# A hybrid decoder trunk on one core: the first two FFN chunks interleaved, x on another queue, idle matmuls at the start, and GpSimd off the tensor work

## The chip, the cores and the metric

The kernel runs on one NeuronCore of a Trainium2 chip. The metric is the device time of one execution in microseconds (us); less is better. Everything is computed in float32, with the large matmuls done in float32r on pairs of high and low parts.

## The reference

Two layers over a sequence of 256 tokens with 1024 features; each adds four sub-layers to h:

```python
h += 0.5 * SwiGLU_1(rms(h))                # 1024 -> 2 x 2816 -> 1024
h += W_out [ A | B | C ](rms(h) @ W_in)    # parallel head groups:
#  A: gated DeltaNet, 4 heads x 128: causal conv on q/k/v, per-head decay,
#     a triangular inverse in each chunk of 64
#  B: dilated sliding-window attention, 4 heads x 64
#  C: causal spatial gating, 4 groups x 64: layer_norm(v), tril(w) @ v, times u
h += CrossAttn(rms(h), rms(mem))           # 4 heads into 256 memory tokens
h += 0.5 * SwiGLU_2(rms(h))
```

A last RMSNorm follows the second layer. The sub-layer with A, B and C is called the mixing stage here.

## The kernel before

**Data.** h is kept transposed: four tiles `hP` (rows `one<-xT`) of two 128-feature blocks by 256 tokens. The weights stream from HBM in pieces of 128x1024 float32 (`wr`, four buffers). `wsplit` makes each piece into a high part `wh` by a ScalarE cast and a low part `wl` by a subtraction, on VectorE or, where the caller says so, on GpSimd. `gained` does the same for x: `X` holds both parts of one 128-feature block times its gain, eight blocks for eight k tiles. `mm2` takes two matmuls for a k tile: `wh` against both parts of X (512 columns) and `wl` against the high part (256). Where parts can't be paired, three matmuls of 256 do it. Results land in PSUM tiles `pg` (four banks, `gbank`) or `ps` (four banks, `sbank`).

**The FFN.** 22 chunks of 128 hidden features. A chunk has a gate half and an up half of eight k tiles each, so 16 pairs of matmuls. `pend` holds two chunks ahead; `evac` reads a chunk's PSUM, applies the row factors `rbh` and SiLU, and splits the product. The row factors come from `Stats`: ScalarE squares (`t<-one`), VectorE adds them up, a matmul with ones sums over partitions (`ps<-one,t`, 128x1), VectorE makes `rv`, GpSimd takes the power -0.5 (`rch<-rv`), VectorE refines it, and a matmul spreads it over the partitions (`ps<-one,rch`).

**The start.** All loads are on SyncE's queue: the gains, then x and the first chunk's weights by turns. The first chunk alone is done k tile by k tile (`wi[0] == 0`); its weights are laid out for that on the host.

**Mixing.** After the row factors come the scalars of the decay (`zz`, `po`, small VectorE rows), six convolution tiles (`xs`, then three VectorE passes into each `q`), norms of k and q, the matrices `M`, and a triangular inverse by doubling: for each of five levels a mask product `Mb<-mc`, four 64x64 matmuls (`tc,Mb`), ScalarE copies to `Q`, four more matmuls (`Q,uc`), subtractions into `tc` and transposes into `uc`. While that runs, TensorE has the projections of the other branches to do. GpSimd does one of the two `wl` of six projections (`pair(x, (None, GP))`), the ten `Mb`, the decay matrices times `qrk`, the layer norm's gain and bias, the mask of the spatial weights, the division in B, the gain of A's output (`L_ZG`) and, later, the low parts of the memory keys.

**The order of the work** is made by `Plan.schedule`: every operation is recorded by a helper (so all rows show line 369 before and 378 after) with a duration and a latency, and a list scheduler puts them in order for each engine by the longest path that follows (`tail`) plus a `boost`. Each engine then runs its list in that order. A change of the planner's constants or of a helper therefore moves instructions everywhere. The planner knows that a VectorE operation with two inputs in SBUF (`kind == "2"`) and a GpSimd operation exclude each other (`lock`).

Of the kernel before, what the change touches and what calls it, by code (L numbers as in the profile page):

```python
# [10 lines left out]
F32 = mybir.dt.float32  # L11
# [19 lines left out]
NS_SLOTS = 37  # L31

# [15 lines left out]
S_BA = 96  # L48
NS = S_BA

L_ZG, L_LG, L_LB, L_BS, L_WS = 0, 128, 384, 640, 896
# [84 lines left out]
class Plan:  # L136
# [25 lines left out]
    def add(self, eng, method, args, kw, outs, ins, dur, lat, table=None, kind=None):  # L162
        i = len(self.ops)
        op = dict(i=i, eng=eng, method=method, args=args, kw=kw, dur=dur, lat=lat, table=table, kind=kind,
                  prio=self.boost, tiles=[], preds={}, succs=[])
# [24 lines left out]
    def schedule(self, fixed=None):  # L190
# [29 lines left out]
        free = {e: 0.0 for e in self.engines}  # L220
# [8 lines left out]
        lock = {"DVE": 0.0, "GP": 0.0}  # L229
        dmas = [o["i"] for o in ops if o["eng"] == "DMA"]  # L230
# [44 lines left out]
        while left:  # L275
            best = None
            for e, lst in ready.items():
# [39 lines left out]
            if e == "DMA":  # L317
                dma_next += 1
                feed = max(feed, t + self.FLIGHT) + lat
                lat = feed - t  # L320
            if e == "PE":
                t += switch(o)
                kind = o["kind"]
            if o["kind"] == "2":
                lock[e] = t + dur
            ready[e].remove(o)
# [147 lines left out]
class Queue:  # L474
    def __init__(self, plan):
        self.plan = plan

    def dma_start(self, o, i):
        n = 1
        for k in o.shape:  # L480
            n *= k
        self.plan.add("DMA", "dma_start", (o, i), {}, [o], [i], Plan.ISSUE, n * 4 / Plan.FEED)


def trunk(tc, xT, memT, w, w2, ca_d, cb_d, sm_d, fin_d, lb_d, out):
    plan = Plan(tc)
    PE, ACT, DVE, GP, SY = Tensor(plan), Scalar(plan), Vector(plan, "DVE"), Vector(plan, "GP"), Queue(plan)
    with ExitStack() as ctx:
# [48 lines left out]
        def cbs(c, n=P):  # L537
            return cb[:, c:c + n]
# [21 lines left out]
        def wchunk(engs=(None, None), cut=1):  # L560

            res = []
            for i in range(2):
                if wi[0] == 0:
                    raw = first[i]
                else:
                    raw = plan.tile([P, HC], F32, "wr", NRAW)
                    SY.dma_start(raw[:, 0:1024], w[2 * wi[0] + i])
                res.append(wsplit(raw[:, 0:1024], engs[i], max(cut // 2, 1)))
            wi[0] += 1  # L570
            return res
# [65 lines left out]
        class Stats:  # L637
# [3 lines left out]
            def add(self, src, last=False):  # L641
                plan.boost = 40.0
# [10 lines left out]
            def finish(self, tag, scales=(1.0,)):  # L653


                plan.boost = 40.0
# [26 lines left out]
        class Norm:  # L683
# [4 lines left out]
            def add(self, d, first=False):  # L688
# [6 lines left out]
                self.st.add(h[d], self.g is None and d == KD - 1)  # L695

        def ffn(norm, nxt, start=False, between=None):
# [3 lines left out]
            def mats(j):  # L701
                wt = wchunk(cut=4 if start and j == 0 else 1)
                pp = [gbank([2, T]) for _ in range(2)]
                if start and j == 0:
                    for k in range(KD):
                        for i in range(2):
                            mm2(pp[i], wt, k // 2 * 512 + i * 256 + k % 2 * P, x[k], k == 0, k == KD - 1)
                    return pp
# [27 lines left out]
            for j in range(2, KF):  # L736
# [83 lines left out]
        def mem_keys(xm):  # L820
            rb = mem_r[1][0]
            KT = []
            for c in range(4):
# [3 lines left out]
                KT.append(parts(k, GP))  # L827
# [15 lines left out]
        def mixing(l, norm, nxt, xm):  # L843
# [10 lines left out]
            pk0 = pair(x, (None, GP))  # L854
# [62 lines left out]
            def conv(n, ps0=None):  # L917
                res = []
                for c in range(2):
                    ps = ps0 if ps0 is not None and c == 0 else pair(x, (None, GP))  # L920
# [213 lines left out]
            for t in (1, 0):  # L1134
                nk = P * (t + 1)
                for par in range(2):
# [14 lines left out]
                    GP.tensor_tensor(p, p, bcl(den, nk), op=ALU.mult)  # L1151
# [35 lines left out]
            GP.tensor_tensor(wsm, lb[:, L_WS:L_WS + 512].rearrange("p (a b) -> p a b", a=4),  # L1187
                             bc4(cbs(C_TRIU)), op=ALU.mult)
            ps = sbank([2, T])
            for t in range(2):  # L1190
# [9 lines left out]
                DVE.tensor_scalar(gv_[:, t, :], gv_[:, t, :], mv[:, 0:1], rs, op0=ALU.subtract, op1=ALU.mult)  # L1200
                GP.tensor_tensor(gv_[:, t, :], gv_[:, t, :], lb[:, L_LG:L_LG + T], op=ALU.mult)
                GP.tensor_tensor(gv_[:, t, :], gv_[:, t, :], lb[:, L_LB:L_LB + T], op=ALU.add)
# [17 lines left out]
            for t in range(2):  # L1220
# [6 lines left out]
                GP.tensor_tensor(z, z, bc4(lb[:, L_ZG:L_ZG + P]), op=ALU.mult)  # L1227
# [5 lines left out]
            for c in range(2):  # L1233
# [4 lines left out]
                sh, sl = parts(ps)  # L1238
# [79 lines left out]
def _pack(a):  # L1318
# [4 lines left out]
    ins["xT"] = f["x"][0].reshape(T, KD, P).transpose(2, 1, 0)  # L1323
# [18 lines left out]
    for l in range(DEPTH):  # L1342
# [23 lines left out]
        for half in range(2):  # L1366
# [18 lines left out]
    chunks[0] = chunks[0].reshape(P, 2, KD // 2, T).transpose(0, 2, 1, 3).reshape(P, WC)  # L1385
# [44 lines left out]
```

## Time and profile before

| | |
|---|---|
| Time, median of 3 runs | 1286.95 us (1285.84 to 1287.96) |
| Time of the profiled execution | 1287.47 us |
| Its span in the profile | 1285.7 us |
| TensorE busy | 1253.5 us (97%) |
| VectorE busy | 957.5 us (74%) |
| ScalarE busy | 718.4 us (56%) |
| GpSimd busy | 120.8 us (9%) |
| HBM read | 213.78 MB, 167 GB/s over the span |

The span runs from the first to the last instruction of the profiled execution; the 1.8 us between it and the execution's time lie around it. PE is TensorE's matmuls, PEld its weight loads, DVE VectorE, ACT ScalarE, POOL GpSimd, SPq SyncE's queue. A busy share is an average: a matmul that stands alone counts with its whole latency. "PEclk" is the TensorE clock that the chip granted, as a share of full speed.

### The profile page before, as it was taken

How to read it: one execution, taken by the hardware profiler on the slowest of the kernel's cores; microseconds unless marked ns; L12 is line 12 of the kernel's file. 1: busy time of each engine (PE TensorE's matmuls, PEld its weight loads, DVE VectorE, ACT ScalarE, POOL GpSimd, SP SyncE). 2: the span in 40 equal slices, each digit the busy share in tenths (PEclk: the TensorE clock that was granted, in tenths of full speed). 3: DMA queues.
4: the chain of work that ended last, by engine and by line, in shares of the span. 5: the costliest groups of instructions: out<-in, count | busy, mean ns of one | idle time of the engine just before them, and what ended most of it. 6: DMA issues, size and time to landing. Idle time of an engine off the chain costs nothing.

```text
span 1285.7 us, 22163 instructions
## 1 busy us (share of the span) xinstructions
PE 1253.5 (97%) x8376; PEld 1129.8 (88%) x8376; DVE 957.5 (74%) x1711; ACT 718.4 (56%) x1286; POOL 120.8 (9%) x135
## 2 busy tenths in 40 slices
PE   7999999999999999999999999998999999999997
PEld 6888889988998988888988888998899989888886
DVE  6777867987775777777677776699867766777764
ACT  6565745735654565555456565466366455555552
POOL 1000002441300000000000000036022000000000
PEclk9999999999999999999999999999999999999998
DMA  6555764423345455556555566643243544555551
GB/s 223 192 189 199 243 204 162 151 99 115 116 165 164 130 177 186 192 172 202 189 180 189 189 200 201 212 163 103 98 132 118 182 161 130 182 182 195 182 193 68
DMA packets 60874, 216.27 MB, mean 168 GB/s; under 512 B 7136, under 2 KB 7520, under 8 KB 60640
## 3 DMA queue, kind: packets, MB, share of 16 engines
q1 hardware_dynamic: 60768, 214.86, 50.5%
q8 instruction: 66, 1.08, 0.4%
q14 instruction: 40, 0.33, 0.1%
HBM read 213.78 MB, written 1.05 MB: 167 GB/s over the span
## 4 chain that ended last, share of the span: by engine, by line
PE 57%; issue 16%; DVE 7%; ACT 1%; DMA 0%; POOL 0%; POOLq 0%; DVEq 0%; SPq 0%; ACTq 0%
PE pg L369 51%; PE ps L369 6%; DVE wl L369 2%; DVE S L369 1%; DVE uc L369 1%; DVE q L369 1%; DVE tc L369 1%; ACT wh L369 1%; DMA S<-memT 0%; POOL wl L369 0%; DVE xs L369 0%; DVE po L369 0%; DVE zz L369 0%; DVE xmx L369 0%; ACT S L369 0%
## 5 line engine op out<-in xcount | busy, mean ns | idle before, releaser
L369 DVE TENSOR_TENSOR wl<-wr,wh 128x1024 fp32r<-128x1024 f32 (+1 forms) x386 | 479.0, 1242 | 231.1 <-ACT wh L369 230.2
L369 ACT CAST wh<-wr 128x1024 fp32r<-128x1024 f32 (+2 forms) x398 | 415.0, 1044 | 418.2 <-issue 254.4
L369 PE MATMUL pg<-X,wh 128*128 128x512 f32 (+1 forms) x2240 | 635.9, 354 | 6.7 <-DVE t L369 6.5
L369 PE MATMUL pg<-X,wl 128*128 128x256 f32 x1824 | 485.1, 282 | 6.0 <-POOL xs L369 2.6
L369 PEld LDWEIGHTS pg<-X,wh 128*128 128x128 f32 x2240 | 382.2, 189 | 53.6 <-ACT wh L369 6.5
L369 PE MATMUL pg<-S,wh 128*128 128x256 f32 (+1 forms) x1560 | 386.7, 327 | 0.0
L369 PEld LDWEIGHTS pg<-X,wl 128*128 128x128 f32 x1824 | 344.5, 189 | 24.4 <-DVE wl L369 4.1
L369 PE MATMUL pg<-S,wl 128*128 128x256 f32 x1088 | 301.9, 282 | 0.5 <-DVE wl L369 0.5
L369 PEld LDWEIGHTS pg<-S,wh 128*128 128x128 f32 x1560 | 260.2, 189 | 24.9
L369 PEld LDWEIGHTS pg<-S,wl 128*128 128x128 f32 x1088 | 205.0, 188 | 3.9 <-DVE wl L369 1.5
L369 DVE TENSOR_TENSOR t<-t,pg 128x256 f32<-128x256 f32 x204 | 84.1, 415 | 3.4 <-ACT t L369 3.4
L369 ACT COPY t<-pg 128x256 f32<-128x256 f32 x204 | 73.9, 366 | 15.1 <-PE pg L369 15.1
L369 DVE TENSOR_TENSOR t<-t,t 128x256 f32<-128x256 f32 x157 | 66.0, 422 | 10.9 <-ACT t L369 3.0
L369 POOL TENSOR_TENSOR rch<-rv,one 128x2 f32<-128x2 f32 x9 | 7.4, 821 | 631.5 <-DVE rv L369 631.5
L369 DVE TENSOR_TENSOR t<-t,rbh 128x256 f32<-128x256 f32 x116 | 48.4, 420 | 0.9
L369 PE MATMUL pg<-wh,X 128*128 128x264 f32 (+2 forms) x192 | 47.4, 332 | 0.0
L369 PE MATMUL ps<-S,S 128*128 128x256 f32 (+4 forms) x384 | 47.0, 289 | 0.0
L369 PEld LDWEIGHTS ps<-S,S 128*128 128x128 f32 (+2 forms) x384 | 41.4, 178 | 2.6 <-issue 1.0
L369 ACT CAST S<-t 128x256 fp32r<-128x256 f32 x88 | 35.8, 408 | 10.1 <-DVE t L369 10.1
L369 ACT ACTIVATE t<-t 128x256 f32<-128x256 f32 x88 | 36.5, 420 | 7.8 <-DVE t L369 7.7
L369 PE MATMUL pg<-wh,S 128*128 128x512 f32 x128 | 40.6, 393 | 0.0
L369 DVE TENSOR_TENSOR S<-t,S 128x256 fp32r<-128x256 f32 x88 | 36.8, 419 | 1.9 <-ACT S L369 1.9
(175 smaller groups left out, 966.6 us busy)
## 6 DMA issues: line engine op xcount, KB each, us to landing
wr<-w SPq DMA_DIRECT2D x390, 512.0 KB, 3.3
wr<-w SPq DMA_DIRECT2D x4, 528.0 KB, 4.6
S<-memT SPq DMA_DIRECT2D x8, 256.0 KB, 6.4
lb<-lb SPq DMA_DIRECT2D x2, 704.0 KB, 6.5
one<-cb SPq DMA_DIRECT2D x1, 1248.0 KB, 6.1
one<-xT SPq DMA_DIRECT2D x4, 256.0 KB, 5.3
wr<-w SPq DMA_DIRECT2D x4, 256.0 KB, 5.5
out<-S SPq DMA_DIRECT2D x3, 256.0 KB, 2.4
```

Of the source, the lines that this page charges most:

```text
L369: getattr(self.engines[o["eng"]], o["method"])(*[real(a) for a in o["args"]], **{k: real(a) for k, a in o["kw"].items()})
```

## The change

**The start.** x goes on ScalarE's queue, in four contiguous tiles, ahead of ScalarE's table load; SyncE's queue has the gains and then only weights. The weights of chunks 0 and 1 are laid out together on the host: each piece holds two k tiles of both chunks, four blocks of 128 columns each. `two()` does both chunks in one pass over the k tiles, into all four `pg` banks, and the third chunk goes into `ps` banks. Twelve float32 matmuls on a zeroed tile `idle` stand ahead of everything on TensorE. The two k tiles of a piece are needed by all four PSUM tiles.

**GpSimd.** All of its tensor work listed above goes to VectorE, but for the powers and the memsets. The layer norm's two GpSimd steps and one VectorE step become two VectorE steps; the division in B becomes two VectorE rows for each of the four tiles of a layer. The gain of A's output is applied in the split of the transposed result (a ScalarE scale and a VectorE operation that was there).

**The planner.** `HOLD = 2.0` makes it stay with float32r or with float32 on TensorE unless the other is worth more; an accumulating matmul may follow its predecessor at once; VectorE and ScalarE rows of other partitions wait for the row before; the first microseconds have slower transfers and matmuls; the boosts of the statistics change.

```diff
-    HOLD = 0.0
+    BEGIN, RAMP, SLOW, WARM = 0.73, 4.5, 2.6, 7.5
+    HOLD = 2.0
...
+                        if e in rows and rows[e] != o["rows"]:
+                            t = max(t, over[e])
...
-                q["at"] = max(q["at"], end + self.hop(o, q))
+                q["at"] = max(q["at"], t + dur if e == q["eng"] == "PE" else end + self.hop(o, q))
...
-        first = [plan.tile([P, HC], F32, "wr", NRAW) for _ in range(2)]
+        first = [plan.tile([P, HC], F32, "wr", NRAW) for _ in range(4)]
+        plan.boost = 1000.0
         for i in range(4):
-            SY.dma_start(hP[i], xT[:, 2 * i:2 * i + 2, :])
-            c = slice(i % 2 * 512, i % 2 * 512 + 512)
-            SY.dma_start(first[i // 2][:, c], w[i // 2][:, c])
+            SA.dma_start(hP[i], xT[i])
+            for c in ((slice(0, 512), slice(512, 1024)) if i == 0 else (slice(0, 1024),)):
+                SY.dma_start(first[i][:, c], w[i][:, c])
+        idle = one([P])
+        DVE.memset(idle, 0.0)
+        warm = sbank([P])
+        for i in range(WARMUP):
+            PE.matmul(warm, lhsT=idle, rhs=idle, start=True, stop=True)
...
+            def two():
+                pp = [gbank([2, T]) for _ in range(4)]
+                for k in range(KD):
+                    if k % 2 == 0:
+                        wt = wsplit(first[k // 2][:, 0:1024], cut=2 if k == 0 else 1)
+                    for n in range(4):
+                        mm2(pp[n], [wt], k % 2 * 512 + n * P, x[k], k == 0, k == KD - 1)
+                wi[0] = 2
+                return [pp[0:2], pp[2:4]]
...
-            pend = [mats(0), mats(1)]
+            pend = two() + [mats(2, sbank)] if start else [mats(0), mats(1)]
...
-            pk0 = pair(x, (None, GP))
+            pk0 = pair(x)
...
-                GP.tensor_tensor(es, es, bcl(rk[:, 4 * t:4 * t + 4]), op=ALU.mult)
+                DVE.tensor_tensor(es, es, bcl(rk[:, 4 * t:4 * t + 4]), op=ALU.mult)
...
-                    GP.tensor_tensor(mb, Mc[t], bc4(cbs(C_LVL + 64 * (n + 1), 64)), op=ALU.mult)
+                    DVE.tensor_tensor(mb, Mc[t], bc4(cbs(C_LVL + 64 * (n + 1), 64)), op=ALU.mult)
```

What this does to the order shows at three places. On ScalarE, the start of the program before (`one_1` to `one_4` are the four tiles of x, `t` squares, `X` the gained blocks, `wh` casts of weights):

```order
L369 ACT_TABLE_LOAD
L369 ACTIVATE nea_93<-one_6_65 128x4
L369 ACTIVATE t_112<-one_1_75 128x256
L369 ACTIVATE t_115<-one_1_75 128x256
L369 CAST wh_118<-wr_82 128x512
L369 ACTIVATE t_125<-one_2_87 128x256
```

and now:

```order
L378 DMA one_1_63<-xT 128x512
...
L378 DMA one_4_98<-xT 128x512
L378 ACT_TABLE_LOAD
L378 ACTIVATE t_125<-one_1_63 128x256
L378 ACTIVATE t_128<-one_1_63 128x256
L378 ACTIVATE X_132<-one_1_63,one_6_69 128x256
L378 ACTIVATE X_136<-one_2_81,one_6_69 128x256
L378 ACTIVATE t_142<-one_2_81 128x256
L378 CAST wh_145<-wr_83 128x512
```

The first cast of weights, which stood behind two squares of the first tile of x, now stands behind three rows of the first tile and two of the second.

On TensorE in the first layer's inverse, from its first doubling step on, before (`Mb` and `Q` rows are the inverse, `X` rows are projections that fill the time):

```order
L369 MATMUL ps_3124<-tc_77,Mb_3033 64x64 x4
L369 MATMUL ps_3131<-tc_80,Mb_3063 64x64 x4
L369 MATMUL pg_3138<-wh_2980,X_1691 128x256
L369 MATMUL ps_3143<-Q_85,uc_3042 64x64 x4
L369 MATMUL ps_3149<-Q_90,uc_3047 64x64 x4
L369 MATMUL pg_3138<-wl_3017,X_1691 128x256
L369 MATMUL pg_3138<-wh_2980,X_1691 128x256
L369 MATMUL pg_3138<-wh_2980,X_1747 128x256
L369 MATMUL ps_3164<-tc_77,Mb_3072 64x64 x4
L369 MATMUL ps_3174<-tc_80,Mb_3081 64x64 x4
```

and now:

```order
L378 MATMUL ps_3202<-tc_85,Mb_3130 64x64 x4
L378 MATMUL ps_3209<-tc_89,Mb_3136 64x64 x4
L378 MATMUL pg_3195<-X_1775,wh_3052 128x256 x2
L378 MATMUL pg_3195<-X_1775,wl_3061 128x256
...
L378 MATMUL pg_3195<-X_1933,wh_3052 128x256
L378 MATMUL ps_3234<-Q_96,uc_3112 64x64 x4
L378 MATMUL ps_3239<-Q_104,uc_3118 64x64 x4
L378 MATMUL pg_3195<-X_1933,wh_3052 128x256
...
L378 MATMUL pg_3195<-X_2071,wl_3061 128x256
L378 MATMUL ps_3259<-tc_85,Mb_3148 64x64 x4
```

Between the first `Mb` step and its `Q` step stood one projection matmul and now seven; up to the second `Mb` step it was three and is eight.

On GpSimd in the first layer's mixing, before (`wl` low parts, `rch`, `brs` powers):

```order
L369 TENSOR_TENSOR rch_2248<-rv_2243,one_12_63 128x2
L369 TENSOR_TENSOR wl_2262<-wr_2124,wh_2246 128x1024
L369 TENSOR_TENSOR wl_2354<-wr_2193,wh_2335 128x1024
L369 MEMSET xs_2450 128x3
L369 TENSOR_TENSOR wl_2461<-wr_2288,wh_2417 128x1024
```

and now:

```order
L378 TENSOR_TENSOR rch_2260<-rv_2255,one_16_67 128x2
L378 MEMSET xs_2483 128x3
L378 MEMSET xs_2542 128x3
L378 MEMSET xs_2551 128x3
L378 MEMSET xs_2578 128x3
```

The six `wl` of this stage are gone from GpSimd's list and stand in VectorE's.

## Rows read from the trace of the kernel before

**Rows 1.** The page, part 1: busy us, share of the span, instructions.

```profile
PE 1253.5 (97%) x8376; PEld 1129.8 (88%) x8376; DVE 957.5 (74%) x1711; ACT 718.4 (56%) x1286; POOL 120.8 (9%) x135
```

**Rows 2.** Busy time by stretch; the first row names the columns.

```profile
core 0: us, PE busy (x) PEld busy (x) DVE busy (x) ACT busy (x) POOL busy (x), PEclk, DMA share, GB/s
0.00:24.70 24.70, 17.52 (x72) 14.30 (x73) 15.82 (x36) 12.99 (x25) 4.77 (x22) 1.00 0.72 241
...
204.10:267.90 63.80, 61.71 (x522) 61.01 (x520) 59.72 (x138) 40.27 (x72) 34.32 (x35) 1.00 0.43 141
267.90:294.80 26.90, 24.49 (x245) 21.72 (x244) 22.49 (x58) 9.90 (x25) 2.83 (x5) 1.00 0.33 110
...
832.80:896.80 64.00, 61.47 (x521) 60.93 (x519) 59.35 (x134) 41.48 (x73) 33.30 (x29) 1.00 0.43 141
896.80:925.60 28.80, 25.82 (x244) 23.07 (x244) 24.36 (x62) 9.89 (x25) 6.17 (x7) 0.94 0.31 101
```

**Rows 3.** Timeline of PE, start: begin, length, instruction, count, idle before.

```profile
6.52 1.22 PE L369 MATMUL pg<-X,wh 128*128 128x512 f32 x2 [6.52 <-DVE t L369]
...
10.42 1.06 PE L369 MATMUL pg<-X,wh 128*128 128x512 f32 x2
...
16.68 1.01 PE L369 MATMUL pg<-X,wh 128*128 128x512 f32 x2
...
18.00 0.63 PE L369 MATMUL pg<-X,wh 128*128 128x512 f32 x2
...
24.50 0.63 PE L369 MATMUL pg<-X,wh 128*128 128x512 f32 x2
...
27.31 0.63 PE L369 MATMUL pg<-X,wh 128*128 128x512 f32 x2
```

**Rows 4.** Timelines of DVE and ACT at the start.

```profile
5.27 0.35 DVE L369 TENSOR_SCALAR X<-one,one 128x256 fp32r<-128x256 f32 x1 [5.27 <-DMA one<-xT]
...
7.24 0.35 DVE L369 TENSOR_SCALAR X<-one,one 128x256 fp32r<-128x256 f32 x1 [0.75 <-DMA one<-xT]
...
5.18 0.72 ACT L369 ACTIVATE t<-one 128x256 f32<-128x256 f32 x2 [2.52 <-DMA one<-xT]
5.85 0.62 ACT L369 CAST wh<-wr 128x512 fp32r<-128x512 f32 x1
...
7.87 0.49 ACT L369 ACTIVATE X<-one,one 128x256 fp32r<-128x256 f32 x1
```

**Rows 5.** Busy time by stretch at the start, columns as in group 2.

```profile
6.00:8.00 2.00, 1.22 (x2) 0.50 (x2) 1.25 (x4) 1.23 (x4) 0.00 (x0) 1.00 0.98 343
```

**Rows 6.** Timeline of DVE in the first layer's mixing.

```profile
212.40 2.37 DVE L369 TENSOR_SCALAR zz<-ex 128x8 f32<-128x8 f32 x1
...
220.19 2.38 DVE L369 SCALAR_TENSOR_TENSOR po<-po,z 128x8 f32<-128x8 f32 x1
...
225.43 0.16 DVE L369 SCALAR_TENSOR_TENSOR po<-po,z 128x8 f32<-128x8 f32 x1
...
228.86 2.79 DVE L369 TENSOR_TENSOR wl<-wr,wh 128x1024 fp32r<-128x1024 f32 x1
231.57 4.19 DVE L369 SCALAR_TENSOR_TENSOR q<-xs,one,q 128x256 f32<-128x256 f32 x5
...
236.35 1.21 DVE L369 TENSOR_TENSOR wl<-wr,wh 128x1024 fp32r<-128x1024 f32 x1
237.49 2.85 DVE L369 SCALAR_TENSOR_TENSOR q<-xs,one,q 128x256 f32<-128x256 f32 x7
...
240.93 3.92 DVE L369 TENSOR_TENSOR wl<-wr,wh 128x1024 fp32r<-128x1024 f32 x2
```

**Rows 7.** Timeline of POOL in the same stretch.

```profile
220.06 2.49 POOL L369 TENSOR_TENSOR wl<-wr,wh 128x1024 fp32r<-128x1024 f32 x1
```

**Rows 8.** Groups of DVE instructions: shapes, count, then busy us, mean ns.

```profile
L369 DVE TENSOR_TENSOR t<-t,t 128x256 f32<-128x256 f32 x157 | 66.0, 422 | 10.9 <-ACT t L369 3.0 <-DVE t L369 0.5
L369 DVE TENSOR_TENSOR S<-S,ps 128x512 f32<-128x512 f32 x17 | 11.1, 678 | 0.3 <-PE ps L369 0.2
```

More of the change, by code (lines that the diff above doesn't have):

```diff
@@ L31 @@
 NS_SLOTS = 37
+WARMUP = 12
 C_ID, C_ONE = 0, 128
@@ L47 @@
 S_DT, S_AL = 88, 92
-S_BA = 96
-NS = S_BA
-L_ZG, L_LG, L_LB, L_BS, L_WS = 0, 128, 384, 640, 896
+S_ON = 96
+NS = 97
+L_LG, L_LB, L_BS, L_WS = 0, 256, 512, 768
 NL = L_WS + 512
@@ L164, in add @@
         op = dict(i=i, eng=eng, method=method, args=args, kw=kw, dur=dur, lat=lat, table=table, kind=kind,
-                  prio=self.boost, tiles=[], preds={}, succs=[])
+                  prio=self.boost, tiles=[], preds={}, succs=[], rows=outs[0].box()[0:2] if isinstance(outs[0], View) else None)
         for views, wr in ((ins, False), (outs, True)):
@@ L219, in schedule @@
                 o["rank"] = r
-        free = {e: 0.0 for e in self.engines}
+        free = {e: self.BEGIN for e in self.engines}
         ready = {e: [] for e in self.engines}
@@ L229, in schedule @@
         lock = {"DVE": 0.0, "GP": 0.0}
+        rows, over = {"DVE": None, "ACT": None}, {"DVE": 0.0, "ACT": 0.0}
         dmas = [o["i"] for o in ops if o["eng"] == "DMA"]
@@ L316, in schedule @@
                 table = o["table"]
-            if e == "DMA":
-                dma_next += 1
-                feed = max(feed, t + self.FLIGHT) + lat
+            if o["method"] == "dma_start":
+                dma_next += e == "DMA"
+                feed = max(feed, t + self.FLIGHT) + lat * (self.SLOW if feed < self.RAMP else 1.0)
                 lat = feed - t
+            if e == "PE" and t < self.WARM:
+                dur, lat = 2 * dur, 2 * lat
             if e == "PE":
@@ L325, in schedule @@
                 lock[e] = t + dur
+            if e in rows:
+                rows[e], over[e] = o["rows"], t + lat + 0.02
             ready[e].remove(o)
@@ L474, with __init__ @@
 class Queue:
-    def __init__(self, plan):
-        self.plan = plan
+    def __init__(self, plan, eng="DMA"):
+        self.plan, self.eng = plan, eng
     def dma_start(self, o, i):
@@ L481, in dma_start @@
             n *= k
-        self.plan.add("DMA", "dma_start", (o, i), {}, [o], [i], Plan.ISSUE, n * 4 / Plan.FEED)
+        self.plan.add(self.eng, "dma_start", (o, i), {}, [o], [i], Plan.ISSUE, n * 4 / Plan.FEED)
 def trunk(tc, xT, memT, w, w2, ca_d, cb_d, sm_d, fin_d, lb_d, out):
@@ L558, in wsplit, with wchunk @@
             return hi, lo
-        def wchunk(engs=(None, None), cut=1):
+        def wchunk(engs=(None, None)):
             res = []
             for i in range(2):
[L564 to L569, printed above, removed]
+                raw = plan.tile([P, HC], F32, "wr", NRAW)
+                SY.dma_start(raw[:, 0:1024], w[2 * wi[0] + i])
+                res.append(wsplit(raw[:, 0:1024], engs[i]))
             wi[0] += 1
@@ L639, in __init__, with add @@
                 self.acc, self.last = None, None
-            def add(self, src, last=False):
-                plan.boost = 40.0
+            def add(self, src, last=False, boost=40.0):
+                plan.boost = boost
                 sq = tmp()
@@ L653, in finish @@
             def finish(self, tag, scales=(1.0,)):
[L656 removed]
+                plan.boost = 60.0
                 ps = sbank([2 + 2 * P])
@@ L694, in add @@
                     act(self.x[-1][:, d % 2, :], h[d], AF.Copy, scale=fin[:, d:d + 1])
-                self.st.add(h[d], self.g is None and d == KD - 1)
+                self.st.add(h[d], self.g is None and d == KD - 1, 5.0 if first else 40.0)
         def ffn(norm, nxt, start=False, between=None):
@@ L699, in ffn, with mats @@
             g, rows = [], []
[L701 to L708, printed above, removed]
+            def two():
[7 more added lines that the diff above has]
+                return [pp[0:2], pp[2:4]]
+            def mats(j, bank=gbank):
+                wt = wchunk()
+                pp = [bank([2, T]) for _ in range(2)]
                 for half, k in ([(i, k) for i in range(2) for k in range(KD)] if j else
@@ L731, in evac @@
                 g.append((sl[:, 0, :], sl[:, 1, :], sl))
-            pend = [mats(0), mats(1)]
+            pend = two() + [mats(2, sbank)] if start else [mats(0), mats(1)]
             rows.extend(norm.st.finish("h", (1.0, 0.5))[1])
             rbh = rows[1]
-            for j in range(2, KF):
+            for j in range(len(pend), KF):
                 plan.boost = 6.0 if j >= KF - 3 else 0.0
@@ L826, in mem_keys @@
                 DVE.tensor_tensor(k, ps, bc4(rb, 2), op=ALU.mult)
-                KT.append(parts(k, GP))
+                KT.append(parts(k))
             return KT
@@ L919, in conv @@
                 for c in range(2):
-                    ps = ps0 if ps0 is not None and c == 0 else pair(x, (None, GP))
+                    ps = ps0 if ps0 is not None and c == 0 else pair(x)
                     for e in range(2):
@@ L1150, in mixing @@
                     DVE.reciprocal(den, den)
-                    GP.tensor_tensor(p, p, bcl(den, nk), op=ALU.mult)
+                    for i in range(2):
+                        DVE.tensor_scalar(p[:, i, :], p[:, i, :], den[:, i:i + 1], None, op0=ALU.mult)
                     for i in range(2):
@@ L1237, in mixing @@
                         PE.transpose(ps[:, e, tsl(t)], zg[t][:, 2 * c + e, :], ident)
-                sh, sl = parts(ps)
+                g = smc[:, S_ON:S_ON + 1]
+                sh, sl = S([2, T], F32R), S([2, T], F32R)
+                act(sh, ps, AF.Copy, scale=g)
+                DVE.scalar_tensor_tensor(sl, ps, g, sh.bitcast(F32), op0=ALU.mult, op1=ALU.subtract)
                 merged[2 * c:2 * c + 2] = [(sh[:, i, :], sl[:, i, :]) for i in range(2)]
```

20 lines of the change are left out of this document (11 added, 9 removed).

## The prediction

> **What bounds the kernel now.** I read the page first, then busy time by stretch, then the timelines of the stretches in which TensorE is not full, and last the two programs' order. TensorE is busy 1253.5 us [rows 1] of a span of 1285.7: 32.2 us are idle, and no more than these and its slow minutes can be won. The order shows where the change can act. TensorE's list differs at the start, in the memory part of the first FFN and in both mixing stages; in cross attention, the later FFNs and the last chunk the same rows follow each other, so the 9 us after the last FFN matmul stay.
>
> The start: by 24.7 us TensorE was busy 17.5 [rows 2]. Its first matmul begins at 6.52, and two matmuls of 512 columns take 1.06 us at 10.42, 1.01 at 16.68, but 0.63 at 18.00 [rows 3]: each 512 took 0.43, then 0.23. The granted clock stands at 1.00 there, but the pitch is that of the 1.2 GHz level until about 17.5 and of 2.4 GHz after. From 24.50 to 27.31 one half of a chunk passes, 8 pairs in 2.81 us [rows 3], so a matmul of 256 columns costs 0.117. The third chunk begins at 24.7.
>
> The mixing stages have two such stretches each. The first runs from the statistics to the first doubling step (204.1 to 267.9, and 832.8 to 896.8); VectorE is busy 59.7 of 63.8 us, TensorE 61.7. The second is the doubling itself (to 294.8, and to 925.6), TensorE 24.5 of 26.9 and 25.8 of 28.8, the last one with a clock of 0.94 [rows 2].
>
> **The start, costed.** Twelve float32 matmuls on zeros stand ahead of the data: even at 0.43 each, the price of a 512 at the lower clock [rows 3], they take 5.2 us from about 1 us on and end before any data can be used, so they cost nothing. What sets the first real matmul is ScalarE. The second tile of x served its first row at 7.24 before [rows 4]; it had 0.8 MB ahead of it with its own bytes. Now two queues move by turns, and 1.05 MB go by then: 0.25 MB more at 343 GB/s [rows 5] is 0.7 later, while issuing from the head of a queue gains some tenths. I take 7.5, bounds 7.0 and 8.0. Behind it ScalarE does a gained block (0.49), a square (0.36) and the cast of half a piece (0.62) [rows 4], less overlap: first matmul at 8.8 instead of 6.52. VectorE then has, ahead of the last of the four pieces' low parts, 4 gains at 0.35 [rows 4], 8 remainders at 0.41, 3 low parts at 1.21 and 2 halves at 0.7 [rows 6], 4 sums at 0.42 [rows 8]: 11.4 us, from the first tile of x (5.3 [rows 4]) plus 1 us of wait for the second tile, so 17.7. The third piece's low part is ready 1.2 earlier, at 16.5, and from there TensorE has two pieces left, 16 pairs or 5.6 us, and 0.4 for the statistics: 22.5. That is 2.2 ahead of 24.7; two small matmuls come later than before, so I book 2.0. If the clock is at its lower level for the first two pieces, up to 3.6 of the twice 2.8 us shows; if x and weights land 0.5 sooner and VectorE waits nowhere, it is 4.5. Bounds -1.6 and +4.5.
>
> The Trainium skill (Trainium Kernel Development and Optimization, Key Constraints) says that transfers issued from different engines run on the same 16 DMA engines and interleave, so that a second issuing engine only saves issue time. The trace agrees: the engines were 0.98 busy from 6 to 8 us with one queue [rows 5]. A queue with room of its own would bring the second tile 1.0 us sooner and the gain of all parts from 11.4 to 12.4; by the rule it stays at 11.4.
>
> **GpSimd off the data, costed.** Per layer, in the first stretch, six low parts, two decay products, the layer norm's steps and six `Mb` come to VectorE. What goes with them: a VectorE row beside a GpSimd row is held until that row ends. `po` with 8 elements takes 2.38 us at 220.19, beside a GpSimd low part of 2.49 from 220.06 [rows 6, 7], and 0.16 alone [rows 6]. In the first layer: `zz` 2.2 too long, `po` 2.2, one `wl` 2.79 for 1.21, five `q` 4.19 for 5 x 0.41, two `wl` 3.92 for 2.4 [rows 6]: 9.6 us together, smaller ones not counted. What comes: 6 x 1.14 for the low parts (pitch of 236.35 to 237.49), 6 x 0.42 for `Mb` [rows 8], 2 x 0.68 for the decay products and 2 x 0.42 for the norm: 11.5. Net +1.9 us of VectorE for the same work, and it had 4.1 idle there [rows 2].
>
> The order also puts more into this stretch: 461 matmuls of 256 columns (wider ones counted by columns) instead of 410, a whole projection more, and for it two low parts and three rows of 0.68: 4.3 us of VectorE. So VectorE needs 63.8 + 1.9 + 4.3 - 4.1 = 65.9 if its idle time is filled, 70.0 if not. TensorE needs 61.7 + 51 x 0.117 = 67.7 (67.4 in the second layer). TensorE becomes the bound, with 6.0 us of later work done. Gain 63.8 + 6.0 - 67.7 = 2.1 and 64.0 + 6.0 - 67.4 = 2.6; bounds -0.2 and, since TensorE's busy time holds latencies, 4 each. I leave 0.5 idle in each: 3.7 together.
>
> In the doubling stretch 141 of those matmuls stand instead of 104, 4.3 us. VectorE gets four `Mb`, two low parts and three rows of 0.68 more, 6.0 us, of which 4.4 us of its idle time there [rows 2] can take some: 28.5 to 32.9. TensorE: 24.5 + 4.3 = 28.8. With 0.5 left idle, 26.9 + 4.3 - 29.3 = 1.9, and in the second layer, where now seven projection matmuls lie between the first `Mb` and `Q` steps and the clock should hold, 28.8 + 4.3 - 29.3 = 3.8; bounds -1.7 and +5 each. Together 5.7.
>
> The other GpSimd rows (keys, division, gain of A) lie beside a TensorE that is full, while VectorE is busy 74% over the span [rows 1]; they are booked at nothing. If that cover were gone, the four key parts are 4 x 0.68 per layer.
>
> **HOLD and the boosts.** In the order, 77 changes from float32r to float32 stand where there were 103. No row gives the price of a change by itself. As an estimate it is no dearer than one matmul of 256 columns, 0.117 [rows 3], so 26 are worth 0 to 3.0, and part of that lies in the stretches above; a statistic held back could cost as much. I book none.
>
> **Sum.** 2.0 + 3.7 + 5.7 = 11.4 us off the profiled execution's 1287.47, which is 0.04% over the median: 1276.
>
> **The rivals.** (1) *The clock does not stay up.* After the twelve matmuls TensorE has some 2.5 us with nothing before the first data. In the second doubling stretch, where TensorE is thin, the clock is 0.94 [rows 2]. Then the start loses its 2.0 and up to 1.6 more: 1278 to 1280.
> (2) *VectorE is the bound in the mixing stages.* It is 94% busy now, and its order is denser by 6 us in each stretch. At 70.0 and 32.9 the four stretches give back all 9.4 us and lose 1.7 (-0.2, 0.0, -1.7 and +0.2): 1287.5 - 2.0 + 1.7 = 1287; with half of its idle time filled 1283. So 1283 to 1288. For it: the chain of waits runs through VectorE there. Against it: the 4 us idle in each stretch, and low parts that come in 1.2 us rather than 2.5.
> (3) *Slower: VectorE's added rows add up in full.* If the long rows are not GpSimd's doing, the 9.6 us stay, and the first stretch takes 63.8 + 11.5 + 4.3 = 79.6, 9.8 us lost against its 6.0 of moved work. Twice that, less 2.0 and 5.7: 1299. It decides as soon as the stretch passes 73.7. Against it: the overlong rows end with GpSimd's rows to 0.1 us.
> (4) *More than I book.* TensorE's stretches had more room than its busy time shows (104 matmuls at 0.117 and 64 small ones do not fill 26.9 us), the changes of type count, and the start reaches its 4.5: 1264 to 1272.
>
> **How the numbers follow.** Forecast 0.45, (4) 0.17, (1) 0.13, (2) 0.14, (3) 0.11. The range 1264 to 1286 leaves out (3), a part of (2) and what is beyond (4). Below 0.2%, about 2.6 us, a measurement of this kernel can't tell from no change: 1284.4 to 1289.5. Faster: the forecast, (4), (1) and 0.04 of (2), 0.79; same: the rest of (2), 0.10; slower 0.11. The forecast's own range is 1272 to 1280.
>
> **What will show it.** In the changed profile: the first real matmul near 8.8, matmuls of 512 at 0.23 from then on, the third chunk at 22.5 instead of 24.7; no `po`, `zz` or `wl` row longer than 1.3 us in mixing; 67 to 69 us between the statistics and the first `Mb` and 28 to 31 for the doubling; clock 1.00 in both. I am wrong if the start's first pieces run at 0.43 per 512, if VectorE is full over both stretches while TensorE waits for `wl`, or if some stretch that the order leaves alone has moved.

## The result: 1268.19 us, 1.5% faster

The changed kernel takes 1268.19 us (median of 4 runs, 1267.80 to 1268.92) against 1287.34 for the kernel before on the same chip (4 runs): ratio 0.9854, 95% interval 0.9837 to 0.9871. The forecast was 1276.0 with a range of 1264 to 1286: the direction and the range hold, the gain is 19.1 us where 11.4 were booked, and the time lies below the 1272 to 1280 that the prediction gave as the forecast's own.

The profile after, the busy times of the engines as in [rows 1]; the span is 1267.1 us:

```profile
PE 1249.3 (99%) x8400; PEld 1128.6 (89%) x8400; DVE 955.6 (75%) x1777; ACT 722.9 (57%) x1289; POOL 26.5 (2%) x69
```

TensorE's idle time fell from 32.2 to 17.8 us and its busy time by 4.2 although it has the twelve idle matmuls more (24 of the count); VectorE is as busy as before. The stretches that answer to [rows 2], statistics to first `Mb` product and then the doubling, in both layers:

```profile
core 0: us, PE busy (x) PEld busy (x) DVE busy (x) ACT busy (x) POOL busy (x), PEclk, DMA share, GB/s
0.00:21.64 21.64, 18.32 (x93) 15.30 (x93) 14.82 (x29) 12.69 (x24) 3.59 (x22) 1.00 0.78 269
202.40:269.60 67.20, 67.20 (x573) 67.03 (x571) 62.20 (x160) 44.42 (x77) 7.23 (x17) 1.00 0.45 150
269.60:297.10 27.50, 27.50 (x238) 23.08 (x237) 24.69 (x69) 13.20 (x28) 0.00 (x0) 1.00 0.37 118
823.70:891.20 67.50, 67.50 (x573) 67.12 (x571) 62.22 (x160) 45.55 (x78) 5.82 (x13) 1.00 0.46 149
891.20:918.70 27.50, 27.50 (x237) 23.08 (x237) 24.70 (x69) 13.20 (x28) 0.00 (x0) 1.00 0.38 118
```

TensorE is full in all four, VectorE has 2.8 to 5.3 us to spare in each. Of VectorE's overlong rows [rows 6] none is left in the first layer's stretch: no single row there is above 1.3 us, and the five `q` that took 4.19 take half of it, 0.41 a row:

```profile
231.60 2.07 DVE L378 SCALAR_TENSOR_TENSOR q<-xs,one,q 128x256 f32<-128x256 f32 x5
```

The start, TensorE's timeline against [rows 3]: the idle matmuls, the first real one, the level of 0.35 for a pair of 512 and 256 columns (8.10 to 8.45), a wait for ScalarE, the third chunk.

```profile
1.05 5.49 PE L378 MATMUL ps<-one 128*128 128x128 f32 x24 [1.05 <-DVE one L378]
6.94 0.73 PE L378 MATMUL pg<-X,wh 128*128 128x512 f32 x2 [0.40 <-ACT wh L378]
...
8.10 0.39 PE L378 MATMUL pg<-X,wh 128*128 128x512 f32 x1
...
8.45 0.39 PE L378 MATMUL pg<-X,wh 128*128 128x512 f32 x1
...
9.72 0.98 PE L378 MATMUL pg<-X,wh 128*128 128x512 f32 x3 [0.76 <-ACT wh L378]
...
21.64 0.39 PE L378 MATMUL ps<-X,wh 128*128 128x512 f32 x1
```

ScalarE and VectorE there, against [rows 4]: the first tile of x is used at 3.72, the second at 5.57, and the cast that the first matmul waits for stands behind both.

```profile
3.72 0.35 DVE L378 TENSOR_SCALAR X<-one,one 128x256 fp32r<-128x256 f32 x1 [2.72 <-DMA one<-xT]
...
5.57 0.51 ACT L378 ACTIVATE X<-one,one 128x256 fp32r<-128x256 f32 x1 [0.52 <-DMA one<-xT]
5.57 0.35 DVE L378 TENSOR_SCALAR X<-one,one 128x256 fp32r<-128x256 f32 x1 [0.97 <-DMA one<-xT]
...
6.29 0.60 ACT L378 CAST wh<-wr 128x512 fp32r<-128x512 f32 x1
```

Where the 18.6 us of the span come from, by marks on TensorE's timeline (the matmuls of the statistics, the `Mb` products), with work that was moved at 0.116 for 256 columns: up to the mixing's statistics 204.1 to 202.4, 1.7. First stretches 2.5 and 2.4: 3.4 and 3.5 us longer with 51 matmuls more, worth 5.9. Doubling: 26.9 to 27.5 and 28.8 to 27.5 with 37 more (4.3): 3.7 and 5.6. From there to the statistics of cross attention 80.8 to 70.1 and 70.0 with 88 fewer (10.2): 0.5 and 0.6. Cross attention 0.5 and 0.6; the rest, and rounding, 0.5. So the two mixing stages give 15.3.

### The profile page after: what moved, and what is told of

It reads as the page before. It is cut to its first block, busy times and chain, and to the rows that moved or that the text cites. A ratio compares the mean times of both kernels' runs of the same rounds, so it can differ in the third digit from the quotient of the medians.

```text
span 1267.1 us, 22194 instructions
## 1 busy us (share of the span) xinstructions
PE 1249.3 (99%) x8400; PEld 1128.6 (89%) x8400; DVE 955.6 (75%) x1777; ACT 722.9 (57%) x1289; POOL 26.5 (2%) x69
## 4 chain that ended last, share of the span: by engine, by line
PE 76%; issue 15%; DVE 4%; DMA 2%; ACT 2%; ACTq 0%; SPq 0%; POOLq 0%; POOL 0%; DVEq 0%
PE pg L378 69%; PE ps L378 7%; DVE S L378 2%; DVE wl L378 2%; ACT S L378 1%; ACT wh L378 1%; DMA wr<-w 1%; DMA one<-xT 1%; DMA one<-cb 0%; DMA S<-memT 0%; DVE t L378 0%; ACT L378 0%; ACTq L378 0%; DVE xmx L378 0%; ACT t L378 0%
## 5 line engine op out<-in xcount | busy, mean ns | idle before, releaser
L378 DVE TENSOR_TENSOR wl<-wr,wh 128x1024 fp32r<-128x1024 f32 (+2 forms) x397 | 484.7, 1222 | 229.4 <-ACT wh L378 228.3
L378 PE MATMUL pg<-X,wh 128*128 128x512 f32 (+1 forms) x2224 | 627.6, 353 | 2.1 <-ACT wh L378 2.1
L378 PE MATMUL pg<-X,wl 128*128 128x256 f32 x1808 | 478.5, 281 | 1.1 <-DVE wl L378 0.9
L378 PEld LDWEIGHTS pg<-X,wh 128*128 128x128 f32 x2224 | 378.3, 188 | 49.2 <-ACT wh L378 3.0
L378 PEld LDWEIGHTS pg<-X,wl 128*128 128x128 f32 x1808 | 339.9, 188 | 18.1 <-DVE wl L378 3.7
L378 ACT CAST S<-t 128x256 fp32r<-128x256 f32 x88 | 35.8, 407 | 10.2 <-DVE t L378 10.2
L378 ACT ACTIVATE t<-one 128x256 f32<-128x256 f32 x72 | 29.5, 412 | 8.6 <-DVE one L378 7.7
```

The costliest lines, as they stand in the source:

```text
L378: getattr(self.engines[o["eng"]], o["method"])(*[real(a) for a in o["args"]], **{k: real(a) for k, a in o["kw"].items()})
```

## The experiments

Three theories were set up after the comparison. Theory A: GpSimd's rows held up VectorE's, and their end made the gain in mixing. Theory B: the planner's new rules made it. Theory C: each needs the other. The kernels of each group ran on one chip together with the kernel before; the kernel after did so on another chip. The kernel before took 1286.67 to 1287.34 us on these chips, so that differences between groups are good to some tenths.

**One of the three parts undone, or one alone.**

The kernel after_gp_back has all of GpSimd's tensor work back, as in

```diff
-            pk0 = pair(x)
+            pk0 = pair(x, (None, GP))
...
-                    DVE.tensor_tensor(mb, Mc[t], bc4(cbs(C_LVL + 64 * (n + 1), 64)), op=ALU.mult)
+                    GP.tensor_tensor(mb, Mc[t], bc4(cbs(C_LVL + 64 * (n + 1), 64)), op=ALU.mult)
```

> The kernel after, with GpSimd's tensor work put back as it was (weight splits, Mb, E, softmax products, gains) and everything else kept: start, planner's model, HOLD 2.0. Theory A, GpSimd's rows held up VectorE and their results came late, and this made the 15.3 us in the two mixing stages: 1281 to 1284 us, first stretch of mixing about 2 us longer, VectorE rows over 2 us beside GpSimd's again. Theory B, the planner's new rules (HOLD 2.0, the wait on changed rows, products issued back to back) made the 15 us by packing TensorE's filler work better: 1268 to 1271 us, both mixing stages as in the kernel after. Theory C, each half is needed for the other: 1272 to 1280 us here and also with the planner's rules undone.

The kernel after_start_back has the old loads, layout and first chunk, and no idle matmuls:

```diff
-            pend = two() + [mats(2, sbank)] if start else [mats(0), mats(1)]
+            pend = [mats(0), mats(1)]
```

> The kernel after with the old start: x and weights by turns on SyncE's queue, chunk 0 alone, no idle matmuls, no pause model for the first transfers. GpSimd's move and the planner's rules stay. Theory A and B: the start is worth what the trace shows of it, third chunk 24.7 instead of 21.6 less 0.45 of small products that were done by then: 1270.5 to 1271.5 us. Rival: what is won at the start is given back in the next 180 us, where weights and VectorE's low parts come just in time: 1268 to 1269 us.

The kernel after_planner_back has the old rules, and the statistics' boost at 40 instead of 60:

```diff
-    HOLD = 2.0
+    HOLD = 0.0
...
-                        if e in rows and rows[e] != o["rows"]:
-                            t = max(t, over[e])
...
-                q["at"] = max(q["at"], t + dur if e == q["eng"] == "PE" else end + self.hop(o, q))
+                q["at"] = max(q["at"], end + self.hop(o, q))
```

> The kernel after with the planner's rules as before: HOLD 0.0, no wait on changed rows, products after products on TensorE with the old lag, statistics' finish at 40 instead of 60. Start and GpSimd's move stay. Theory A: 1268 to 1271 us, of which up to 3.0 is float32 and float32r switching (103 switches each way instead of 77). Theory B: 1280 to 1284 us. Theory C: 1272 to 1280 us.

The kernel before_gp_off is the kernel before with the first of these diffs reversed.

> The kernel before with only GpSimd's tensor work moved to VectorE and ScalarE as in the kernel after: old start, old planner. Theory A: 1271 to 1274 us, nearly the whole gain but the start. Theory B: 1285 to 1288 us, no gain without the rules. The third rival of the prediction (VectorE's added rows add up on its path unless the planner's order makes room): 1288 to 1299 us. Theory C: 1275 to 1284 us.

Measured, with TensorE's idle and busy time (page, part 1; idle is span less busy) and the time from the mixing's statistics to those of cross attention in the two layers:

| kernel | us | ratio to before (95%) | TensorE idle, busy | mixing, two layers |
|---|---|---|---|---|
| before | 1287.34 | 1 | 32.2, 1253.5 | 171.4, 173.6 |
| after | 1268.19 | 0.9854 (0.9837 to 0.9871) | 17.8, 1249.3 | 164.8, 165.0 |
| after_gp_back | 1287.46 | 1.0004 (0.9995 to 1.0013) | 31.6, 1254.0 | 174.8, 173.9 |
| after_start_back | 1269.17 | 0.9859 (0.9846 to 0.9873) | 20.7, 1246.8 | 164.6, 164.9 |
| after_planner_back | 1279.47 | 0.9937 (0.9925 to 0.9950) | 23.0, 1254.4 | 169.5, 169.5 |
| before_gp_off | 1278.75 | 0.9934 (0.9920 to 0.9948) | 27.5, 1249.4 | 169.3, 169.1 |

Theories A and B both fall. C fits after_planner_back and before_gp_off; after_gp_back, at 1287.46, is slower than all three expected: with GpSimd's rows nothing is left of the gain. GpSimd's move alone is worth 8.2 us (1286.97 on that chip to 1278.75); the planner's rules add 9.6 and 11.3 to it (1278.75 to 1269.17 with the old start, 1279.47 to 1268.19 with the new one) and nothing without it, since the kernel with the rules and the new start but with GpSimd's rows is as slow as the one before. The start is worth 1.0 at most (1269.17 lies between the two ranges expected), within the spread, and nothing under the old rules. With GpSimd's work back, the first stretch and the doubling of the first layer:

```profile
201.20:266.20 65.00, 61.81 (x520) 61.15 (x519) 59.03 (x132) 39.73 (x70) 28.92 (x31) 1.00 0.44 143
266.20:299.30 33.10, 31.39 (x270) 27.24 (x270) 28.13 (x71) 12.88 (x29) 6.95 (x9) 0.95 0.31 103
```

TensorE is not full in either, and VectorE's long rows are back beside GpSimd's, here those of VectorE, then GpSimd's:

```profile
217.21 2.37 DVE L378 SCALAR_TENSOR_TENSOR po<-po,z 128x8 f32<-128x8 f32 x1
```

```profile
217.08 2.47 POOL L378 TENSOR_TENSOR wl<-wr,wh 128x1024 fp32r<-128x1024 f32 x1
```

With the old rules but without GpSimd the doubling stretch has 78 matmuls of 256 columns and TensorE waits in it for `tc`, `uc`, `Q` and `S` (kernel after_planner_back):

```profile
266.40:290.00 23.60, 21.56 (x210) 18.32 (x211) 22.48 (x66) 9.00 (x24) 0.00 (x0) 1.00 0.29 90
```

**Is it exclusion or lateness?** Two kernels add GpSimd rows whose result nobody reads to the kernel after, behind each mixing's statistics. In the first TensorE, VectorE and ScalarE have the same rows in the same order as in the kernel after.

Rows that read, kernel after_gp_reads:

```diff
+            sp, sq = spare.unsqueeze(1), cbs(0, 1024).unsqueeze(1)
+            for i in range(12):
+                plan.add("GP", "tensor_tensor", (sp, sq, bcl(r[:, 0:1], 1024)), dict(op=ALU.mult),
+                         [sp], [sq, r], 2.34, 2.38)
```

> The kernel after, with twelve GpSimd rows more in each mixing stage, right behind the statistics: a product of two tiles in SBUF, 128x1024, into a spare tile that nobody reads. TensorE's, VectorE's and ScalarE's lists are the same rows in the same order as in the kernel after. Theory A, a GpSimd row holds up VectorE's rows beside it: some 29 us of such rows per layer; 34 us cost VectorE 9.6 us in the kernel before, so about 8 us of VectorE in a first stretch where it has 5 idle: the stretch 70 to 75 us instead of 67.2, in all 1274 to 1284 us, with VectorE rows of 2 us and more again. Rival, only GpSimd's late results cost: 1268 to 1269.5 us.

Rows that only write, kernel after_gp_writes:

```diff
+            for i in range(36):
+                plan.add("GP", "memset", (spare, 0.0), {}, [spare], [r], 0.78, 0.80)
```

> The same with rows of GpSimd that only write: 36 fills of the spare tile, 128x1024, in each mixing stage, some 30 us of GpSimd as well; a few rows of VectorE change places. Theory A with the reading port as the thing shared: nobody is held, 1268 to 1270 us. Rival, any GpSimd row of that length costs (its own small rows, the square roots and the fills of xs, come late behind it): 1272 us and more, as with the reading rows.

Measured: reading rows 1299.05 us (ratio 1.0096, 1.0081 to 1.0111), slower than the kernel before; writing rows 1269.0 (0.9863, 0.9848 to 0.9877). The first stretch of the first layer in the two kernels:

```profile
201.80:284.30 82.50, 71.97 (x572) 70.17 (x570) 78.62 (x160) 44.42 (x77) 33.98 (x29) 0.96 0.37 122
```

```profile
200.80:268.50 67.70, 67.46 (x573) 67.08 (x571) 62.86 (x160) 44.63 (x77) 40.58 (x53) 1.00 0.45 149
```

The same 160 rows of VectorE take 78.62 instead of 62.20 us, and the stretch 15.3 more than after's 67.2; twice that is the loss. TensorE's own busy time in it grows from 67.20 to 71.97 for the same matmuls, at a granted clock of 0.96. 33.98 us of GpSimd that read do this, 40.58 that mostly write don't. The rows, VectorE's and then GpSimd's, show who is held, while six of GpSimd's take 2.2 each: a low part of 2.86 instead of 1.22, and products of 8 elements of 1.85; at 210.08 also a step with one tensor input.

```profile
207.30 2.86 DVE L378 TENSOR_TENSOR wl<-wr,wh 128x1024 fp32r<-128x1024 f32 x1
210.08 1.86 DVE L378 TENSOR_SCALAR zz<-ex 128x8 f32<-128x8 f32 x1
...
214.56 1.85 DVE L378 TENSOR_TENSOR zz<-zz,ex 128x8 f32<-128x8 f32 x1
```

```profile
205.20 13.17 POOL L378 TENSOR_TENSOR one<-one,rch 128x1024 f32<-128x1024 f32 x6 [1.80 <-DVE rch L378]
```

So GpSimd's rows are shown to cost by holding VectorE, without any result that comes late; whether late results cost something besides in the kernel before was not tested. The hold is not their whole length: 26.8 us of GpSimd more in the stretch cost VectorE 16.4. The loss is larger than expected (1274 to 1284). A likely reason, not tested, is that in the kernel before the planner places VectorE's rows around GpSimd's, while here it doesn't know of them. The Trainium skill (SBUF — State Buffer, Who interferes with whom) says that VectorE with two SBUF inputs contends with a GpSimd instruction that reads SBUF, not with one that only writes it. The two kernels agree: 16.4 us of VectorE against 0.7 in one stretch.

**The planner's rules one by one, and the idle matmuls.** Of the diff of after_planner_back the kernel after_hold0 takes the first piece alone, after_rows_back the second and after_pepe_back the third, each from the kernel after. In after_warm0

```diff
-WARMUP = 12
+WARMUP = 0
```

> The kernel after with HOLD 0.0 alone; all else kept. Its order has 76 matmuls of 256 columns inside the doubling stretch, as with all the planner's rules undone (78), against 141, and 474 against 461 ahead of it. Theory A, HOLD's place for filler in the doubling chain is what the rules are worth: a stretch that covers the chain takes 26.6 us with 141 of them, one that does not 22.7 with 78, so 3.4 us a layer go, and with the later stretch's 1.2: 1275 to 1278 us, waits for tc, uc, Q and S on TensorE back to 0.1 to 0.4 each. Theory B, HOLD is worth its changes of type only (85 each way instead of 77): 1268.5 to 1270 us. Theory C, the rows rule (VectorE's and ScalarE's wait on changed partitions) holds the chain: 1268 to 1269 us here.

> The kernel after, with only the planner's rule for products that follow products on TensorE as before (the old lag, -0.2 us from the end). Both stretches of mixing keep their 461 and 141 matmuls of 256 columns; in the last one there are 43 changes of type instead of 25, over the program 97 each way instead of 77. Theory A and the switch price read at the start (0.09 us one way, less the other): 20 more pairs at about 0.11, 1270 to 1271 us. Rival, a change costs nothing where the engine is full: 1268 to 1269 us. Rival, dearer, since each change also breaks a run of products: 1272 to 1275 us.

> The kernel after, without the planner's rule that a row of VectorE or ScalarE on other partitions waits for the one before it. The order has 432 matmuls of 256 columns ahead of the doubling and 170 inside it, against 461 and 141, the later stretch the same 412. Theory A: the doubling is covered either way, 1267.5 to 1269.5 us. Theory C, this rule is what made the chain fit: 1272 to 1279 us.

> The kernel after without the twelve idle matmuls. Theory A, the level of the clock at the start is set by what TensorE did before: the first 512-column matmuls take about 0.43 each instead of 0.23 to 0.35, the third chunk starts 1 to 3 us later than 21.6, and as the memory part takes back 1.6 of the start's 2.6 us (the old start costs only 1.0 in all): 1268.5 to 1270 us. Rival, the idle matmuls do nothing: third chunk within 0.3 of 21.6, 1267.8 to 1268.6 us.

| kernel | us | ratio to before (95%) | TensorE idle, busy | mixing, two layers |
|---|---|---|---|---|
| after_hold0 | 1271.86 | 0.9885 (0.9871 to 0.9898) | 19.5, 1250.9 | 167.9, 165.2 |
| after_pepe_back | 1272.71 | 0.9892 (0.9879 to 0.9906) | 19.5, 1251.5 | 166.0, 166.3 |
| after_rows_back | 1277.51 | 0.9937 (0.9923 to 0.9952) | 21.8, 1253.7 | 168.8, 170.5 |
| after_warm0 | 1268.19 | 0.9856 (0.9843 to 0.9870) | 21.5, 1244.7 | 164.8, 164.9 |

Theory A was wrong on which rule counts: undoing HOLD costs 3.7 us and not 7 to 10, which none of its three ranges has, and undoing the rule for rows, which A expected to cost nothing, costs 9.3 by the medians (its five runs go from 1276.72 to 1280.35). The three undone singly cost 17.5, together 11.3: they are settings of one list and don't add. For the product rule (1272.71, the range of the dearer rival), 20 more pairs of type changes go with 2.2 us of TensorE's busy time, 0.11 a pair; the rest is idle time (waits for VectorE's `S` 4.0 instead of 0.9). That is no price of a change: with HOLD 0.0, 8 more pairs go with 1.6 us, 0.2 a pair.

What the rule for rows does is seen in the doubling on VectorE's timeline. In the kernel after, the steps of the two token tiles stand together, eight transposes in 2.03 us:

```profile
272.47 1.16 DVE L378 TENSOR_TENSOR tc<-tc,ps 64x128 f32<-64x128 f32 x4
273.66 2.03 DVE L378 STREAM_TRANSPOSE uc<-tc 32x128 f32<-32x128 f32 x8
```

Without the rule each tile goes by itself, four in 1.25:

```profile
272.27 0.59 DVE L373 TENSOR_TENSOR tc<-tc,ps 64x128 f32<-64x128 f32 x2
272.88 1.25 DVE L373 STREAM_TRANSPOSE uc<-tc 32x128 f32<-32x128 f32 x4
```

and the stretch takes 33.9 us with TensorE busy 32.03, for 170 matmuls of 256 columns instead of 141. It is not the number of rows that stand together: without the rule a row of eight is no faster.

```profile
281.01 2.55 DVE L373 STREAM_TRANSPOSE uc<-tc 32x128 f32<-32x128 f32 x8
```

It is which rows are neighbours: in the kernel after, the eight of 273.66 go in pairs, 0.23 to 0.24 us apart within a pair and 0.27 to 0.28 between pairs, and the four of 272.88 are 0.31 to 0.32 apart.

With the 256-column matmuls taken out of the doubling stretch at 0.116 each, the rest is the chain and its waits:

| kernel | doubling, first layer | matmuls of 256 | rest | second layer, rest |
|---|---|---|---|---|
| before | 26.9 | 104 | 14.8 | 16.7 |
| before_gp_off | 23.9 | 78 | 14.8 | 14.9 |
| after_planner_back | 23.9 | 78 | 14.9 | 14.9 |
| after_rows_back | 33.9 | 170 | 14.2 | 14.2 |
| after_gp_back | 33.0 | 148 | 15.9 | 14.6 |
| after_hold0 | 20.7 | 76 | 11.8 | 11.8 |
| after | 27.5 | 141 | 11.2 | 11.2 |

So the rule for rows and the move of GpSimd's work shorten the chain by some 3 us a layer only where both are there, with HOLD or without. That is what theory C says. How much of it is shorter rows on VectorE and how much the two tiles' products standing together on TensorE was not separated.

Without the idle matmuls TensorE starts at the lower level, 0.43 for a 512 up to 11.1, and has the third chunk at 21.00, no later than with them:

```profile
7.12 1.22 PE L378 MATMUL pg<-X,wh 128*128 128x512 f32 x2 [7.12 <-ACT wh L378]
...
8.57 0.63 PE L378 MATMUL pg<-X,wh 128*128 128x512 f32 x1
9.00 0.41 PE L378 MATMUL pg<-X,wl 128*128 128x256 f32 x1
9.21 0.63 PE L378 MATMUL pg<-X,wh 128*128 128x512 f32 x1
...
11.89 1.08 PE L378 MATMUL pg<-X,wh 128*128 128x512 f32 x4
...
21.00 0.39 PE L378 MATMUL ps<-X,wh 128*128 128x512 f32 x1
```

The clock is raised by the idle matmuls, as theory A said, but TensorE then waits for casts and low parts: the data set the pace of the first pieces. The time, 1268.19, is the same, as the rival expected.

**x on SyncE's queue, and a larger HOLD.**

In the kernel after_xsync

```diff
-            SA.dma_start(hP[i], xT[i])
+            SY.dma_start(hP[i], xT[i])
```

> The kernel after with x issued on SyncE's queue again, by turns with the weights in the same order and sizes; nothing goes out from ScalarE. If transfers from two engines share the same 16 engines and a second queue only saves issue time, x's first tile is used some tenths later than 3.72 and the second some tenths later than 5.57, the third chunk starts within 0.7 of 21.64: 1268 to 1269 us. Rival, the second queue gave the bytes: second tile at 7 or later, as before and as the prediction had it, first real matmul at 8 to 9, third chunk 1 to 2 us later: 1268.5 to 1270 us.

and in after_hold25

```diff
-    HOLD = 2.0
+    HOLD = 2.5
```

> The kernel after with HOLD 2.5 instead of 2.0, a try at a faster one. 76 changes of type each way instead of 77, the same 461 and 142 matmuls ahead of and inside the doubling. If the stretches are full already, 1267.5 to 1269 us; if the order behind the doubling closes some of the 3 us of waits that are left in the memory part and the mixing, 1265 to 1267.5 us.

HOLD 2.5 takes 1267.79 us (0.9852, 0.9835 to 0.9868): the same, the stretches are full. x on SyncE's queue takes 1266.37 (0.9841, 0.9827 to 0.9856), less than either range expected, and is the fastest kernel of the study by its median. Its interval overlaps that of the kernel after; its runs, 1265.79 to 1267.08, lie below all of the kernel after and just below those of after_hold25 on the same chip (1267.12 to 1268.11). ScalarE's timeline in the kernel after (first row its queue):

```profile
0.73 1.86 ACTq L378 DMA_DIRECT2D one<-xT  x4
...
2.63 1.28 ACT L378 ACT_TABLE_LOAD   x1 [2.63 <-issue]
...
3.92 0.72 ACT L378 ACTIVATE t<-one 128x256 f32<-128x256 f32 x2
...
9.06 0.60 ACT L378 CAST wh<-wr 128x512 fp32r<-128x512 f32 x1
```

and with x on SyncE's queue:

```profile
0.73 1.28 ACT L378 ACT_TABLE_LOAD   x1 [0.73 <-PEq L1447]
...
3.95 0.51 ACT L378 ACTIVATE X<-one,one 128x256 fp32r<-128x256 f32 x1 [1.22 <-DMA one<-xT]
...
4.82 0.62 ACT L378 CAST wh<-wr 128x512 fp32r<-128x512 f32 x1
...
5.50 0.72 PE L378 MATMUL pg<-X,wh 128*128 128x512 f32 x2
...
6.21 0.62 ACT L378 CAST wh<-wr 128x512 fp32r<-128x512 f32 x1 [0.45 <-DMA wr<-w]
...
7.47 0.35 DVE L378 TENSOR_SCALAR X<-one,one 128x256 fp32r<-128x256 f32 x1
```

Four issues take ScalarE 1.86 us and push its table load from 0.73 to 2.63. That costs next to nothing here: ScalarE's first row on x starts at 3.92 with them and at 3.95 without, since the first tile of x lands no sooner (VectorE uses it at 3.72 and 4.04). What differs is the weights. The two half pieces that come first land 5.3 us after their issue in the kernel after and 3.6 us with one queue (medians, page, part 6):

```profile
wr<-w SPq DMA_DIRECT2D x2, 256.0 KB, 5.3
```

```profile
wr<-w SPq DMA_DIRECT2D x2, 256.0 KB, 3.6
```

In the kernel after their casts also stand behind rows of the second and third tile of x, at 6.29 and 9.06; with one queue they follow the landing, at 4.82 and 6.21. The second tile of x is then used at 7.47 instead of 5.57, but the first piece of weights does not need it, and the first real matmul comes at 5.50 instead of 6.94. How much is the landing and how much the order of ScalarE's list was not separated. The third chunk starts by 19.3 instead of 21.64, and at the mixing's statistics this kernel is at 199.8 against 202.4. Not all of this is the queue's: the profiled execution of the kernel after is the slowest of its four, and after_gp_writes, with the same start, is there at 200.8. The medians differ by 1.8.

## Why the prediction was right, and where its sizes were not

**The bound.** That TensorE becomes the bound in the mixing, with VectorE relieved of GpSimd's long rows, is what the trace shows (67.20 of 67.20 us busy, clock 1.00), and the reading rows confirm the cause by adding it alone. Rivals (2) and (3) rested on VectorE being too full; it has 2.8 to 5.3 us to spare. Rival (4), more than booked, is what happened, though without the 4.5 us that it wanted from the start.

**First stretch, 3.7 booked, 4.9 measured.** The mechanism and the sum of work were right; the 0.5 left idle in each was not there. VectorE's own sum was too high: 65.9 us booked, 62.2 measured.

**Doubling, 5.7 booked, 9.3 measured.** The mis-sized term. I added 4.3 us of moved matmuls to TensorE's busy 24.5 and reached 28.8, and left 0.5 idle; it took 27.5 all told, 1.8 less in each layer, which is the 3.6 missing. I had taken the busy time of the chain as fixed. Without its 256-column matmuls the stretch fell from 14.8 to 11.2 us in the first layer, and with the rule for rows undone it stays at 14.2: that rule was not priced at all.

**HOLD and the planner, booked at 0, bounds 0 to 3.0.** This step failed in its attribution. I read the moved work from the new order, rightly, but counted the rules only for changes of type. Undone together they cost 11.3 us. The sum did not suffer as much, because the stretches were priced with the new order; but GpSimd's move, to which I gave the gain, is worth 8.2 without the rules.

**Start, 2.0 booked, 1.0 at most in the time.** What sets the first real matmul was read rightly, ScalarE's rows behind the second tile of x. That tile was taken at 7.5 and used at 5.57, the first real matmul at 8.8 came at 6.94, and the third chunk at 21.64 instead of 22.5: by itself 3.1 less 0.45 of small products. At the mixing's statistics 1.7 of it are left against the kernel before, and 0.6 against the old start with the new rules (202.4 against 203.0). Why the rest isn't kept stays open, since single executions differ by as much: after_gp_writes and after_gp_reads, with the same start, have the third chunk at 20.94 and 22.38 and the statistics at 200.8 and 201.8. Between 100 and 203 us TensorE is idle for 1.8 in the kernel after, for 0.9 and 0.5 in these two, and for 1.0 with the old start.

Rival (1) is out for this execution, whose pairs take 0.35 from 8.10 on, but not for this start: in the profile of after_gp_reads TensorE waits 1.79 us, and from 10.5 to 14.5 the granted clock is 0.57 and a 512 takes 0.43 again.

```profile
10.50 1.49 PE L378 MATMUL pg<-X,wh 128*128 128x512 f32 x3 [1.79 <-ACT wh L378]
```

**The rule on queues.** I had weighed that by the Trainium skill (Trainium Kernel Development and Optimization, Key Constraints) a second issuing engine only saves issue time, and that transfers interleave. The runs agree that they interleave: with two queues the second tile of x came 1.9 us sooner and the first weights later. The prediction had the second tile at 7.5, behind the 7.24 of the kernel before, and no term for weights that land later.

## What to carry to other kernels

GpSimd rows that read SBUF can hold VectorE's rows beside them until they end (26.8 us of them cost VectorE 16.4); count VectorE's overlong rows before giving GpSimd a share of the work. A planner's rule and the work it orders have to be undone separately and together, since neither is worth what it is worth with the other. At a kernel's start, ask of a second queue which transfers it brings forward and which it puts back: here x came sooner than it was needed, and the weights, which were needed first, came later.

## What the hardware showed that I had not expected

- GpSimd fills (36 of 128x1024 in a layer, 40.6 us of GpSimd in the stretch) left VectorE at 62.9 us where 62.2 was usual; products of the same tile drove it to 78.6.
- At the start the column PEclk reads 1.00 in the kernel without idle matmuls too (8 to 11 us), while its matmuls run at 0.43 for 512 columns: there the pitch tells the level, not the column.
- A row of eight transposes of 32x128 takes 2.03 us in the order that the rule for rows makes and 2.55 in another.
